# Norms of q and k by way of DRAM: the heads' sums spread over 128 partitions for root and reciprocal, and read back as rows

## The chip, the cores and the metric
One core of a Trainium2 chip runs the whole kernel. The metric is device microseconds (us) from start to end; 1604.22 us is the median of three runs before the change.

The engines are PE (TensorE: matmuls; PEld is its weight load), DVE (VectorE), ACT (ScalarE), POOL (GpSimd) and SP (SyncE, which here only issues DMAs). Each takes its instructions strictly in the order of the program; an instruction that waits holds everything behind it on its engine.

## The reference, cut to what matters
Two layers of a hybrid block over 256 latent and 256 context tokens. Each layer projects the normed tokens to an SSD branch, a neighbourhood attention and a gated MLP, merges the three, and ends with a SwiGLU FFN. The change touches the norms of q and k ahead of the attention: 8 heads of 64 channels, each head of each token normed by itself.

```
def rmsnorm(t, w):
    tf = t.astype(jnp.float32)
    tf = tf * lax.rsqrt(jnp.mean(tf * tf, axis=-1, keepdims=True) + EPS)
    return tf.astype(t.dtype) * w

def qkv_heads(t, q_norm, k_norm):
    q, k, v = [u.reshape(Bt, L, NA_HEADS, NA_HEAD_DIM) for u in split_cols(t, (NA_WIDTH,) * 3)]
    return rmsnorm(q, q_norm), rmsnorm(k, k_norm), v
```

All arithmetic is fp32. Layer 0 needs q and k of all 512 tokens, layer 1 (the last) k of all and q of the 256 latent ones.

## The kernel before, in words
Activations lie as channels on partitions and tokens along the free dimension: a tile `T()` is 128 channels by 512 tokens, fp32, and all such tiles share one pool of `N_T` buffers. A tile of q or k holds one pair of heads (64 partitions each), so four tiles hold all eight heads.

Every fp32 product is made of three matmuls in fp32r: each weight tile is split into a high part (`hi`, a cast on ACT, L222) and a remainder (`lo`, a subtraction on DVE, L232), each activation likewise, and `mm3` or `product` adds hi*hi, hi*lo and lo*hi in PSUM. Nearly all matmuls are therefore recorded at line L126, the helper `mm`; the tile names tell them apart (g is a projection's PSUM tile, s that of a small product).

The weights are one stream of 316 tiles of 512 KB. `Stream.get` keeps `hi` two tiles ahead of PE and `lo` one to two; after each `lo`, SP issues the load of the tile three further on (`load_to`, L212) into one of five raw buffers, and waits until that buffer is free.

The order of the instructions is written out by the program as it is traced. PE's projections are the backbone: every four tiles of k (12 matmuls) `gemm` calls `tick`, which lets side work take steps. There are three queues of side work, each a list of generators: "ssd" (the state space branch), "att" (the gated MLP's mixing, the norms of q and k, then the attention) and "mod" (the next modulation vectors). One `yield` is one step; the rate of "att" is 1.0 step a tick until all q, k and v are projected. Work can also be put off by a part of a tick (`later`).

`qk_tile` projects one tile of q or k, copies it from PSUM and squares it on ACT. When the four tiles of one kind are there, `qk_norm(kind)` is put into the "att" queue: once for k and once for q in each layer, four norms in all. `Q_0`, `Q_1` and `Q_2` are numbers of steps that it lets pass, (1, 2), (3, 5) and (6, 3) for layers 0 and 1.

Before the change a norm runs so: four groups of matmuls (L1073) sum the squares of each pair's two heads; pair j's sums land on the 32 partitions from 32j on (repeated, even heads and odd heads alternating). ACT takes the root of the whole 128 x 512 tile (L1076 for q, L1078 for k), DVE the reciprocal in halves of 256 columns, one step of the queue apart (L1081). After `Q_1` steps the result is split into an fp32r part and a remainder held on other partitions (L1086 on ACT, L1087 on DVE), so that one fp32r matmul restores it. After `Q_2` more steps, one step apart for each pair, a matmul with the 0/1 matrix `selp` (L1092, recorded at L126) spreads the pair's two rows over 64 partitions each, in PSUM, and DVE multiplies (L1094).

Two other paths through DRAM exist already and are used below as measures: `Fd` and `Cd` are small DRAM tiles written from the tile R (L869, L871) and read back as rows repeated over partitions, `rb` (L888, 128 partitions) and `ex` (L956, twice 64 partitions of 2 KB).

The attention, which reads q and k first in `stack` (L1109), is put into the queue when the "ssd" queue's last group has ended.

Of the kernel before, what the change touches and what calls it, by code (L numbers as in the profile page):

```python
# [9 lines left out]
F32 = mybir.dt.float32  # L10
F32R = mybir.dt.float32r
BF16 = mybir.dt.bfloat16
AF = mybir.ActivationFunctionType
ALU = mybir.AluOpType
AX = mybir.AxisListType
MUL, ADD, SUB, MAX, MIN = ALU.mult, ALU.add, ALU.subtract, ALU.max, ALU.min
# [17 lines left out]
C_ROW = 1280  # L34
C_BS = 1312
C_SP = 1344
# [2 lines left out]
C_MB = 1488  # L39
NC_ = 1616  # L40

N_T = 61
N_W = 5
LA = 2
N_WARM = 34
# [50 lines left out]
def kernel(ctx: ExitStack, tc: tile.TileContext, a, out):  # L96
    nc = tc.nc
    ctx.enter_context(tc.manual_schedule())
    PE, ACT, DVE, SP = nc.tensor, nc.scalar, nc.vector, nc.sync

    cpool = ctx.enter_context(tc.tile_pool(name="const", bufs=1))
    lpool = ctx.enter_context(tc.tile_pool(name="layer", bufs=2))
    tpool = ctx.enter_context(tc.tile_pool(name="t", bufs=N_T))
    rpool = ctx.enter_context(tc.tile_pool(name="raw", bufs=5))
# [3 lines left out]
    dpool = ctx.enter_context(tc.tile_pool(name="dram", bufs=1, space=bass.MemoryType.DRAM))  # L108
# [3 lines left out]
    def nm(s):  # L112
        cnt[0] += 1
        return f"{s}{cnt[0]}"

    def T(s="t", dt=F32):
        return tpool.tile([128, TOK], dt, tag="t", name=nm(s))

    def S(s="s"):
        return pspool.tile([128, 512], F32, tag="p", name=nm(s))  # L120

    def small(w, tag, bufs=None):
        return spool.tile([128, w], F32, tag=tag, name=nm(tag), bufs=bufs)

    def mm(o, l, r, start=True, stop=True):
        PE.matmul(o, l, r, start=start, stop=stop)  # L126


    cst = cpool.tile([128, C_MF], F32, name="cst")
# [12 lines left out]
    epsb, eps4, eps64 = (eps3[:, i:i + 1] for i in range(3))  # L142
    for e, f in ((epsb, 1.0), (eps4, 4.0), (eps64, 64.0)):
        DVE.memset(e, f * EPS)
    mk = cpool.tile([128, 256], F32, name="mk")
    selp = cpool.tile([128, 8, 128], F32R, name="selp")
    lom = cpool.tile([128, 1], F32, name="lom")
    ident = cst[:, C_ID:C_ID + 128]
    ones = cst[:, C_ONE:C_ONE + 128]

# [124 lines left out]
    def gemm(acts, c0, c1=512, la=LA):  # L275

        nk = len(acts)
        ps = S("g")
        for k, act in enumerate(acts):
            wh, wl = ws.get(pos[0] + k, la=la)  # L280
            product(ps, wh, wl, act, c0, c1, k == 0, k == nk - 1)
            if k % KT == KT - 1 or k == nk - 1:
                tick((k % KT + 1) / 4 * (c1 - c0) / 512)
        pos[0] += nk
        return ps
# [89 lines left out]
    def table(func):  # L375

        ACT.activation(dummy, epsb, func)


    class SumSq:  # L380
# [32 lines left out]
        def spread(self, c0, c1):  # L413

            if self.rs is None:
                self.rs = S("rs")
            for i in range(c0 // 128, c1 // 128):
                mm(self.rs[:, i * 128:i * 128 + 128], self.st[:, i:i + 1].to_broadcast([128, 128]), ident)
            return self.rs
# [74 lines left out]
    for k in range(8):  # L494
        t = T("x")
# [21 lines left out]
    h = [(T("hh", F32R), T("hl", F32R), 0) for _ in range(8)]  # L517
# [87 lines left out]
    for l in range(NL):  # L605
# [5 lines left out]
        def pcol(c, n=1):  # L611
            return P[:, c:c + n]
# [24 lines left out]
        for i in range(4):  # L637
            if last:
                t, c = ysc.norm(pl[i])
                ACT.activation(t[:, lat], t[:, lat], AF.Gelu_apprx_tanh, bias=c)  # L640
            else:
                t = T("u")
                ACT.activation(t, pl[i], AF.Gelu_apprx_tanh)
            u.append(t)
        if not last:
            SP.dma_start(out=cst[:, 0:C_ONE], in_=a["cst"][:, 0:C_ONE])
            SP.dma_start(out=cst[:, C_COS:C_ROW], in_=a["cst"][:, C_COS:C_ROW])
            SP.dma_start(out=cst[:, C_BS:C_MF], in_=a["cst"][:, C_BS:C_MF])
            SP.dma_start(out=mk, in_=a["cst"][:, C_MF:NC_])
            DVE.tensor_copy(selp.rearrange("p a (b c) -> p a b c", c=64),  # L650
                            cst[:, C_SP:C_SP + 16].rearrange("p (a b) -> p a b", b=2).unsqueeze(3).to_broadcast(
                                [128, 8, 2, 64]))

            DVE.tensor_reduce(out=lom, in_=cst[:, C_ROW + 4:C_ROW + 8], op=ADD, axis=AX.X)
            DVE.tensor_scalar(lom, lom, -1.0, None, MUL)

        def token_major(n0, evac, between=()):

# [113 lines left out]

        Fd = dpool.tile([64, 2, 128], F32, name=nm("Fd"))
        Cd = dpool.tile([16, 4, 128], F32, name=nm("Cd"))

        def pair_rows(j, pr):

            return selp[:, 2 * j + pr]

        def dt_gen():  # L780
            for _ in range(D_0[l]):
# [284 lines left out]
        def qk_norm(kind):  # L1066

            b = 0 if kind == "k" else c0
            for _ in range(Q_0[l]):
                yield  # L1070
            ps = S()
            for j in range(4):
                mm(ps[32 * j:32 * j + 32, b:], cst[:, C_BS:C_BS + 32], qsq.pop((kind, j))[:, b:])  # L1073
            rq, RQ = T("rq"), T("RQ", F32R)
            if kind == "q":
                ACT.activation(rq[:, b:], ps[:, b:], AF.Sqrt, bias=eps64)  # L1076
            else:
                ACT.activation(rq[:, b:], ps[:, b:], AF.Sqrt, scale=1.0 / 64, bias=epsb)  # L1078
            table(AF.Exp)
            for c in range(b, 512, 256):  # L1080
                DVE.reciprocal(rq[:, c:c + 256], rq[:, c:c + 256])  # L1081
                yield
            for _ in range(Q_1[l]):
                yield

            ACT.copy(RQ[:, b:], rq[:, b:])  # L1086
            DVE.scalar_tensor_tensor(RQ[:, b:], RQ[:, b:].bitcast(F32), lom, rq[:, b:], MUL, ADD)  # L1087
            for _ in range(Q_2[l]):
                yield
            for j in range(4):  # L1090
                ps = S()
                mm(ps[:, b:], pair_rows(j, 0), RQ[:, b:])  # L1092
                t = qk[kind, j]
                DVE.scalar_tensor_tensor(t[:, b:], t[:, b:], pcol(P_KN if kind == "k" else P_QN),  # L1094
                                         ps[:, b:], MUL, MUL)
                yield

        def attention():
# [173 lines left out]
        for g in range(4):  # L1272
            tiles = (g, 4 + g, 8 + 2 * g, 9 + 2 * g)
            if g < 2:
                for j, i in enumerate(tiles):
                    conv_tile(i)
                    qk_tile(j, "kq"[g])
            else:
                conv_tile(tiles[0])
                v_half(g - 2, [lambda: conv_tile(tiles[1])])  # L1280
                conv_tile(tiles[2])
                conv_tile(tiles[3])
            later(L_G[l], lambda g=g: queues["ssd"].append(ssd_group(g)))
            if g < 2:
                queues["att"].append(qk_norm("kq"[g]))
# [41 lines left out]
        for j in range(8):  # L1327
            ps = gemm(h, c0)
            t = T("z")
# [39 lines left out]
        h = None  # L1369
# [41 lines left out]
        for m in range(3, 8):  # L1411
            ps = gemm(mx, c0)
# [83 lines left out]
        if not last:  # L1496
# [9 lines left out]
            for m in range(8):  # L1506
                if m == 7:
                    drain("mod")
                    ysc = Scaled(xn, modA1, l + 1, 0)
                    ps = S("g")  # L1510
# [9 lines left out]
                else:  # L1520
                    ps = gemm(f, 0)
# [4 lines left out]
            h = [(T("hh", F32R), T("hl", F32R), 0) for _ in range(8)]  # L1526
            ysc.add()
        else:
            for m in range(8):

                ps = gemm(f if m < 7 else [tuple(z) for z in f], 256)
# [138 lines left out]
def _build(nc, arrays):  # L1670
    aps = {k: nc.dram_tensor(f"in_{k}", v.shape, mybir.dt.from_np(v.dtype), kind="ExternalInput").ap()
           for k, v in arrays.items()}
    out = nc.dram_tensor("out_0", (128, 8, 256), F32, kind="ExternalOutput").ap()
    with tile.TileContext(nc) as tc:
        kernel(tc, aps, out)
# [12 lines left out]
```

## Time and profile before

| | |
|---|---|
| runs, median of 3 (lowest, highest) | 1604.22 us (1604.22, 1604.6) |
| profiled execution, own time | 1605.74 us |
| its span, first to last instruction | 1603.7 us |
| granted TensorE clock, mean | 0.997 |
| PE busy | 1581.2 us, 99% |
| PEld busy | 1324.2 us, 83% |
| DVE busy | 1162.3 us, 72% |
| ACT busy | 830.3 us, 52% |
| DMA: moved, mean rate | 254.37 MB, 159 GB/s |

Busy time is the sum of the instructions' times on an engine. Matmuls overlap in their pipeline, so what a matmul costs PE is read from the start of one to the start of the next, not from its own duration. "Idle before it" of an instruction is time in which its engine stood still, and the name behind it is what released it; "issue" is time for which the profile shows no such event. A stretch A:B is in us from the span's start. The k norm of layer 0 stands at about 138 to 196 us and its q norm at 195 to 257 us; in layer 1 they stand at about 1098 to 1149 and 1162 to 1208 us.

### The profile page before, as it was taken

Reading aid. Unit: us, or ns where it says so; the run is one execution under the profiler, and the core shown is the slowest. Engines: PE = TensorE matmul, PEld = TensorE weight load, DVE = VectorE, ACT = ScalarE, POOL = GpSimd, SP = SyncE. Lnnn points to the kernel's source line nnn. Section 1 sums busy time; section 2 is a strip of 40 time slices with the busy share of each in tenths; the row PEclk is TensorE's granted clock in tenths of the full one; section 3 lists DMA queues with packets and bytes.
Section 4 is the critical chain, followed back from the end, with each engine's and each line's share of the span. In section 5 each row is a group of like instructions: output and inputs, shape, how many; then the busy total and the mean of one; then the engine's idle time right before and its main releaser. Section 6 shows DMA issues by size and latency. Waiting matters only on the chain.

```text
span 1603.7 us, 23594 instructions
## 1 busy us (share of the span) xinstructions
PE 1581.2 (99%) x8908; PEld 1324.2 (83%) x8909; DVE 1162.3 (72%) x2005; ACT 830.3 (52%) x1551; POOL 6.9 (0%) x21
## 2 busy tenths in 40 slices
PE   9999999999999999999999999999999999999999
PEld 5878787767788888988888888978888989998888
DVE  5477889878968656666666654778988987687664
ACT  4456876646743234433222212658676775566652
POOL 0000000000000000000000000000000000000000
PEclk9999999999999999999999999999999999999999
DMA  9523333443344445455456765425434455656654
GB/s 347 190 61 122 115 107 107 154 153 99 113 130 127 157 144 178 133 171 166 162 184 206 261 231 177 171 93 161 132 118 138 140 158 178 204 163 196 187 173 135
DMA packets 87345, 254.37 MB, mean 159 GB/s; under 512 B 10560, under 2 KB 19008, under 8 KB 87104
## 3 DMA queue, kind: packets, MB, share of 16 engines
q1 hardware_dynamic: 87232, 252.87, 49.3%
q8 instruction: 70, 1.15, 0.3%
q14 instruction: 43, 0.35, 0.1%
HBM read 248.44 MB, written 4.39 MB: 158 GB/s over the span
## 4 chain that ended last, share of the span: by engine, by line
PE 78%; DVE 11%; ACT 5%; DMA 4%; issue 2%; SPq 0%; ACTq 0%; DVEq 0%
PE g L126 70%; PE s L126 6%; DVE lo L232 3%; DVE xbc L718 2%; DMA wm<-in_wmod 1%; ACT hi L222 1%; DMA rb<-Fd 1%; PE s L1186 1%; ACT M L987 1%; DVE scr L192 1%; DMA wr<-in_ws 1%; DVE bt L1141 0%; DVE M L896 0%; ACT rb L987 0%; ACT sw L740 0%
## 5 line engine op out<-in xcount | busy, mean ns | idle before, releaser
L126 PE MATMUL g<-hh,hi 128*128 128x512 f32 (+1 forms) x1280 | 471.0, 368 | 0.0
L126 PE MATMUL g<-hh,lo 128*128 128x512 f32 (+1 forms) x1280 | 462.0, 361 | 1.4 <-DVE lo L232 1.4
L126 PE MATMUL g<-hl,hi 128*128 128x512 f32 (+1 forms) x1280 | 461.8, 361 | 0.5 <-DVE hl L551 0.4
L232 DVE TENSOR_TENSOR lo<-wr,hi 128x1024 fp32r<-128x1024 f32 x316 | 382.5, 1219 | 92.9 <-ACT hi L222 92.7
L222 ACT CAST hi<-wr 128x1024 fp32r<-128x1024 f32 x316 | 323.7, 1046 | 38.8 <-DMA wr<-in_ws 36.0
L126 PEld LDWEIGHTS g<-hh,hi 128*128 128x128 f32 x1280 | 241.5, 189 | 48.7 <-issue 11.9
L126 PEld LDWEIGHTS g<-hh,lo 128*128 128x128 f32 x1280 | 241.5, 189 | 41.1 <-DVE lo L232 3.8
L126 PEld LDWEIGHTS g<-hl,hi 128*128 128x128 f32 x1280 | 241.7, 189 | 37.2 <-DVE hl L551 1.1
L192 DVE SCALAR_TENSOR_TENSOR scr<-wm,csil 128x1024 bf16<-128x1024 f32 x128 | 156.1, 1220 | 55.4 <-DMA wm<-in_wmod 55.4
L126 PE MATMUL g<-hp,hi 128*128 128x512 f32 x304 | 107.6, 399 | 0.0
L718 DVE SCALAR_TENSOR_TENSOR xbc<-g,pv,xbc 128x508 f32<-128x508 f32 (+3 forms) x128 | 91.3, 713 | 9.5 <-ACT xbc L712 6.4
L126 PE MATMUL g<-hp,lo 128*128 128x256 f32 x304 | 85.6, 282 | 0.9 <-DVE lo L232 0.8
L1295 ACT ACTIVATE th<-g,pv 128x512 f32<-128x512 f32 (+1 forms) x48 | 27.9, 581 | 95.3 <-PE g L126 89.6
L367 ACT CAST fh<-f 128x512 fp32r<-128x512 f32 x22 | 13.6, 620 | 112.3 <-DVE f L1446 112.3
L126 PE MATMUL g<-fh,lo 128*128 128x512 f32 x176 | 68.6, 390 | 0.5 <-DVE lo L232 0.5
L126 PEld LDWEIGHTS g<-hp,hi 128*128 128x128 f32 x304 | 57.1, 188 | 14.1
L126 PE MATMUL g<-fh,hi 128*128 128x512 f32 x176 | 68.5, 389 | 0.0
L126 PE MATMUL g<-fl,hi 128*128 128x512 f32 x176 | 68.5, 389 | 0.0
L126 PE MATMUL g<-lo,hh 128*128 128x256 f32 x224 | 63.6, 284 | 3.2 <-DVE lo L232 3.1
L126 PE MATMUL g<-hi,hh 128*128 128x256 f32 x224 | 64.6, 288 | 0.0
L126 PE MATMUL g<-hi,hl 128*128 128x256 f32 x224 | 63.3, 283 | 0.0
L126 PE MATMUL g<-fp,hi 128*128 128x512 f32 (+1 forms) x198 | 62.4, 373 | 0.0
(310 smaller groups left out, 2658.2 us busy)
## 6 DMA issues: line engine op xcount, KB each, us to landing
wr<-in_ws SPq DMA_DIRECT2D x316, 512.0 KB, 4.2
wm<-in_wmod SPq DMA_DIRECT2D x80, 512.0 KB, 4.5
rb<-Fd SPq DMA_DIRECT2D x48, 256.0 KB, 4.0
wm<-in_wm SPq DMA_DIRECT2D x32, 256.0 KB, 6.0
ex<-Cd SPq DMA_DIRECT2D x32, 128.0 KB, 3.8
bias<-in_rpb SPq DMA_DIRECT2D x32, 128.0 KB, 2.1
x<-in_xT SPq DMA_DIRECT2D x8, 256.0 KB, 5.1
xm<-in_xT SPq DMA_DIRECT2D x8, 256.0 KB, 5.5
```

The lines of the kernel that those rows point to most:

```text
L126: PE.matmul(o, l, r, start=start, stop=stop)
L192: DVE.scalar_tensor_tensor(scr, raws[n], 1.0, csil[:, v, :], MUL, MUL, accum_out=modr[l][:, ft, v:v + 1])
L222: ACT.copy(hi, self.raw[i])
L232: DVE.tensor_tensor(lo, self.raw.pop(i), hi, SUB)
L367: ACT.copy(hi, src[:, c0:])
L718: DVE.scalar_tensor_tensor(av3[:, :, o0:o1], pv3[:, :, o0 + d:o1 + d], w(j), av3[:, :, o0:o1], MUL, ADD)
L987: ACT.activation(z, z, AF.Exp, bias=bias(st, d))
L1186: PE.transpose(ps[:, kt * 256 + qt * 128:kt * 256 + qt * 128 + 128], src, ident)
L1295: ACT.activation(th[:, c0:], ps[:, c0:], AF.Tanh, scale=0.5, bias=pcol(P_BG + br * 8 + m))
```

## The change
The heads' sums of squares are copied from PSUM by ACT and written to a DRAM tile `Nd` of 8 heads by n tokens (n is 512, or 256 for q in layer 1), two rows from each group of 32 partitions. They are read back flat as `w`, 128 partitions by n/16 values. After `Q_1` steps the root (ACT) and the reciprocal (DVE) are taken of `w`, which is written to a second DRAM tile `Ni`. `spread(j)` reads the two rows of a pair back, each repeated on 64 partitions, with two DMAs into an SBUF tile; pair 0's is issued at once, pair j+1's just ahead of pair j's multiplication. The multiplication reads that tile in place of PSUM. The matmuls with `selp`, the split into two parts, `selp` and `lom` themselves and their set-up are gone, and so is the step between the two halves of the reciprocal. The tile pool has one buffer more (4 KB of `selp` are free).

```diff
-N_T = 61
+N_T = 62
...
-    selp = cpool.tile([128, 8, 128], F32R, name="selp")
-    lom = cpool.tile([128, 1], F32, name="lom")
...
-            rq, RQ = T("rq"), T("RQ", F32R)
-            if kind == "q":
-                ACT.activation(rq[:, b:], ps[:, b:], AF.Sqrt, bias=eps64)
-            else:
-                ACT.activation(rq[:, b:], ps[:, b:], AF.Sqrt, scale=1.0 / 64, bias=epsb)
-            table(AF.Exp)
-            for c in range(b, 512, 256):
-                DVE.reciprocal(rq[:, c:c + 256], rq[:, c:c + 256])
-                yield
+
+            n = 512 - b
+            t, w = T("rq"), small(32, "rqs", 2)
+            Nd, Ni = (dpool.tile([8, n], F32, name=nm("Nd")) for _ in range(2))
+            ACT.copy(t[:, b:], ps[:, b:])
+            for j in range(4):
+                SP.dma_start(out=Nd[2 * j:2 * j + 2], in_=t[32 * j:32 * j + 2, b:])
+            flat = lambda z: z.rearrange("h t -> (h t)").rearrange("(p c) -> p c", p=128)
+            w = w[:, 0:n // 16]
+            SP.dma_start(out=w, in_=flat(Nd))
             for _ in range(Q_1[l]):
                 yield
-
-            ACT.copy(RQ[:, b:], rq[:, b:])
-            DVE.scalar_tensor_tensor(RQ[:, b:], RQ[:, b:].bitcast(F32), lom, rq[:, b:], MUL, ADD)
+            if kind == "q":
+                ACT.activation(w, w, AF.Sqrt, bias=eps64)
+            else:
+                ACT.activation(w, w, AF.Sqrt, scale=1.0 / 64, bias=epsb)
+            table(AF.Exp)
+            DVE.reciprocal(w, w)
+            SP.dma_start(out=flat(Ni), in_=w)
+            R = {}
+
+            def spread(j):
+                R[j] = T("RQ")
+                for a_ in (0, 1):
+                    SP.dma_start(out=R[j][64 * a_:64 * a_ + 64, b:],
+                                 in_=Ni[2 * j + a_].unsqueeze(0).to_broadcast([64, n]))
+
+            spread(0)
             for _ in range(Q_2[l]):
                 yield
             for j in range(4):
-                ps = S()
-                mm(ps[:, b:], pair_rows(j, 0), RQ[:, b:])
                 t = qk[kind, j]
+                if j < 3:
+                    spread(j + 1)
                 DVE.scalar_tensor_tensor(t[:, b:], t[:, b:], pcol(P_KN if kind == "k" else P_QN),
-                                         ps[:, b:], MUL, MUL)
+                                         R.pop(j)[:, b:], MUL, MUL)
                 yield
```

## Rows read from the trace of the kernel before

**Rows 1.** Page, part 1: busy us, share of the span, instructions by engine.
```profile
PE 1581.2 (99%) x8908; PEld 1324.2 (83%) x8909; DVE 1162.3 (72%) x2005; ACT 830.3 (52%) x1551; POOL 6.9 (0%) x21
```
**Rows 2.** Page, part 4: the chain that ended last, by engine.
```profile
PE 78%; DVE 11%; ACT 5%; DMA 4%; issue 2%; SPq 0%; ACTq 0%; DVEq 0%
```
**Rows 3.** Stretches: length, then busy us of each engine, clock, DMA share, GB/s.
```profile
150.00:176.00 26.00, 26.00 (x115) 20.24 (x114) 19.50 (x34) 19.20 (x46) 0.00 (x0) 1.00 0.56 174
176.00:192.00 16.00, 16.00 (x77) 11.94 (x76) 15.76 (x27) 13.98 (x35) 0.00 (x0) 1.00 0.43 146
200.00:230.00 30.00, 30.00 (x175) 24.64 (x174) 26.09 (x43) 22.12 (x57) 0.00 (x0) 1.00 0.36 109
230.00:250.00 20.00, 17.82 (x104) 14.39 (x103) 19.35 (x30) 12.65 (x28) 0.00 (x0) 1.00 0.50 154
...
1098.00:1130.00 32.00, 31.19 (x192) 26.36 (x192) 29.36 (x47) 28.79 (x64) 0.00 (x0) 1.00 0.64 198
```
**Rows 4.** Tile RQ: count, ns min/median/max, first and last start, forms.
```profile
L126 PE MATMUL s<-RQ,selp x16: 278/486/580, 176.5 to 1206.2; 128*128 128x512 f32 x12, 128*128 128x256 f32 x4
...
L1087 DVE SCALAR_TENSOR_TENSOR RQ<-RQ,lom,rq x4: 476/742/752, 158.4 to 1186.1; 128x512 fp32r<-128x512 f32 x3, 128x256 fp32r<-128x256 f32 x1
```
**Rows 5.** Timeline of PE: start us, us, instruction.
```profile
176.53 0.58 PE L126 MATMUL s<-RQ,selp 128*128 128x512 f32 x1
...
180.82 0.50 PE L126 MATMUL s<-RQ,selp 128*128 128x512 f32 x1
...
181.16 0.40 PE L126 MATMUL g<-hh,hi 128*128 128x512 f32 x1
...
1199.60 0.28 PE L126 MATMUL s<-RQ,selp 128*128 128x256 f32 x1
...
1199.72 0.40 PE L126 MATMUL g<-hh,hi 128*128 128x512 f32 x1
```
**Rows 6.** Timeline: matmuls that PE waited for; idle time and releaser in brackets.
```profile
198.58 0.39 PE L126 MATMUL g<-lo,hh 128*128 128x256 f32 x1 [0.93 <-DVE lo L232]
...
244.91 0.38 PE L126 MATMUL g<-lo,hh 128*128 128x256 f32 x1 [2.18 <-DVE lo L232]
...
253.23 0.47 PE L126 MATMUL s<-RQ,selp 128*128 128x512 f32 x1 [1.34 <-DVE xbc L718]
...
1130.64 0.50 PE L126 MATMUL g<-hh,lo 128*128 128x512 f32 x1 [0.78 <-DVE lo L232]
```
**Rows 7.** Groups on DVE by form: busy us, mean ns, idle before, releaser.
```profile
L730 DVE SCALAR_TENSOR_TENSOR xbc<-ct,xbc 128x512 f32<-128x512 f32 x28 | 19.1, 682 | 0.0
L1081 DVE RECIPROCAL rq<-rq 128x256 f32<-128x256 f32 x7 | 12.2, 1747 | 3.6 <-ACT rq L1078 3.0 <-ACT rq L1076 0.6
...
L1094 DVE SCALAR_TENSOR_TENSOR k<-k,pv,s 128x512 f32<-128x512 f32 x8 | 5.9, 740 | 0.0
...
L1148 DVE RECIPROCAL ast<-ast 128x2 f32<-128x2 f32 x16 | 2.5, 158 | 0.3 <-ACT bt L1144 0.3
```
**Rows 8.** Tile ex, read from DRAM: issue ns on SP, and time to landing.
```profile
L956 SPq DMA_DIRECT2D ex<-Cd x32: 450/587/1480, 160.7 to 1233.1; - x32
...
DMA to landing us min/median/max: 2.7/3.8/8.8
```
**Rows 9.** Tile R, written to DRAM in twelve DMAs: time to landing.
```profile
DMA to landing us min/median/max: 1.4/1.6/1.9
```
**Rows 10.** Timeline of layer 0's k norm: the sums, and the cast five steps later.
```profile
138.61 1.06 PE L126 MATMUL s<-sq,cst 128*32 128x512 f32 x8
...
156.17 0.62 ACT L1086 CAST RQ<-rq 128x512 fp32r<-128x512 f32 x1
```
**Rows 11.** SP's waits in 130:260: us in total, times, longest us.
```profile
SPq L212 <- DVE lo L232: 33.7, 7, 9.4
...
SPq L869 <- ACT R L867: 10.4, 1, 10.4
```
**Rows 12.** Line L1109 in 0:700, the attention's first read of k.
```profile
L1109 ACT CAST ks<-k x8: 610/616/621, 347.3 to 422.8; 64x512 fp32r<-64x512 f32 x8
```

More of the change, by code (lines that the diff above doesn't have):

```diff
@@ L649 @@
             SP.dma_start(out=mk, in_=a["cst"][:, C_MF:NC_])
[L650 to L655, printed above, removed]
         def token_major(n0, evac, between=()):
@@ L774 @@
         Cd = dpool.tile([16, 4, 128], F32, name=nm("Cd"))
-        def pair_rows(j, pr):
-            return selp[:, 2 * j + pr]
         def dt_gen():
```

## The prediction, made before the changed kernel ran
> **What bounds the kernel now.** I began with the busy times: PE is busy 99% of the span, DVE 72% [rows 1]. The chain that ended last says the same, 78% PE, but 11% of it is DVE [rows 2], so DVE must end PE's waits somewhere. The table of stretches shows where. From 176 us on, where layer 0's projections, its SSD groups and these norms run side by side, DVE is busy 15.76 of 16 us, 26.09 of 30 and 19.35 of 20, while PE drops to 17.82 of 20 in the last of these; in layer 1's k norm it is 29.36 of 32 for DVE [rows 3]. The timeline then gives the single waits of PE next to the norms: 0.93, 2.18 and 0.78 us for the remainder of a weight tile, which DVE makes, and 1.34 us of a matmul of the norm itself for a PSUM bank that DVE's convolution taps held [rows 6]. So near the norms there are two bounds close together: PE nearly everywhere, DVE just behind it, and in front at four places worth 5.2 us.
>
> **PE, on the path.** Sixteen matmuls with the selector go, 12 of 512 columns and 4 of 256 [rows 4]. Their durations overlap with their neighbours, so I count from start to start: the one at 180.82 us moves the next matmul to 181.16, that is 0.34 us; a narrow one at 1199.60 moves it to 1199.72, 0.12 us [rows 5]. All sixteen, read that way, lie between 0.12 and 0.36. For the wide ones I take 0.28, for the narrow ones 0.15: 12 x 0.28 + 4 x 0.15 = 4.0 us. The bounds are 16 x 0.12 = 1.9 and 16 x 0.34 = 5.4 us. The sums of squares stay as they are.
>
> **DVE, partly on the path.** A norm of 512 columns loses two reciprocals of 1.747 us [rows 7] and the remainder of 0.742 [rows 4], 4.24 us. It gains one reciprocal of 128 x 32. The profile has 0.158 us for 128 x 2 and 1.747 for 128 x 256 [rows 7]; a straight line between them gives 0.35. The four multiplications read SBUF in place of PSUM; today they take 0.740, and the same operation on SBUF tiles 0.682 (L730) [rows 7], so 0.23 is saved. Net -4.1 us in three norms and about half, -2.1, in layer 1's q: 14.4 us in all. Of that only what ends a wait of PE counts. The 2.18 and the 1.34 us stand late in layer 0's q norm, behind its 4.1 us; the 0.78 stands behind both reciprocals of layer 1's k norm. The 0.93 at 198.58 stands behind multiplications only, and I leave it. So 4.3 us could go, from nothing to all. I take half, 2.2 us, because the new multiplications may wait (below) and because the PSUM bank is wanted by the next product anyway.
>
> **ACT.** A copy replaces the root on the wide tile, a root on a small tile is added, and the cast goes; table loads stay the same in number. That is no more work than before, on an engine with 2 us free in the tightest stretch of 16 [rows 3]: nothing. If the small root has to wait for its data, though, ACT stops, and with it the emptying of PSUM.
>
> **Is `w` there in time?** Copy (about as long as the cast, 0.62 us [rows 10]), four issues on SP, the write's landing, one more issue, the read's landing. With 0.59 us an issue [rows 8], 1.6 for the write [rows 9], and for the read between 1.6 [rows 9] and 3.8 [rows 8] it is 0.6 + 4 x 0.59 + 1.6 + 0.6 + 1.6 to 3.8 = 6.8 to 9.0 us. The cover is Q_1 steps. Layer 0's k norm took five steps from 138.61 to 156.17 [rows 10], 3.5 us each, so three are 10.5 us. It fits by 1.5 us at the narrowest place; layer 1 has five steps. Cost: nothing, and up to 2 us where SP is late.
>
> **SP.** Each norm puts 14 DMAs into the queue that also carries the weights and the SSD rows: 14 x 0.59 = 8.3 us of issue, and two places where SP stands until a DMA of its own has landed, 1.6 us each. Behind them stand weight loads (L212) and the rows rb. The weights have room: in this part SP itself stood 33.7 of 130 us waiting for DVE to free a raw buffer [rows 11]. It has stood before without harm to PE: 10.4 us for the tile R [rows 11], and PE behind it is busy 26.00 of 26 [rows 3]. [...] The rows rb can come later by about two landings; ACT waits for them just once today. I put 0.6 us on this, from 0 to 3.2 (two landings in the one norm, layer 0's k, in which the first rows are fetched).
>
> **Is the spread there in time?** Pair 0's has the Q_2 steps. Pair j+1's is issued one step ahead of its use; steps here are 180.82 - 176.53 = 4.3 us [rows 5], about 4.0 without the matmul. Two issues and a landing like ex, which has exactly this shape, are 2 x 0.59 + 3.8 = 5.0 us [rows 8]. Where SP is level with DVE in the program, DVE waits 1.0 us for it; where SP is ahead, nothing. Twelve such spreads, half of them late: 6 us of DVE, well below the 14.4 that it gains. [...]
>
> **Latency of the norm.** It ends two steps earlier in the program, and k and q of layer 0 are first read at 347.3 us [rows 12], some 90 us after the last multiplication. Hidden; the buffer more and the dropped set-up of `selp`, three DVE instructions once in the whole run, I put at nothing.
>
> **Sum.** -4.0 - 2.2 + 0.6 = -5.6 us. The profiled execution took 1605.74 us around a span of 1603.7; it would become 1600.1. The median of the runs is 1.5 us lower, 1604.22, so I predict 1598.6 us. What a measurement can tell from no change is 0.2%, or 3.2 us: 1601.0 to 1607.4.
>
> **Rivals.**
> More goes: all four waits of PE end, as DVE's 14.4 us would allow. -4.0 - 5.2 = -9.2, 1595.0 us. For it: the waits are short beside what DVE is relieved of. Against it: each wait that goes may show the next one, and spreads cost DVE time.
> DVE stays the bound in layer 0: the eight wide matmuls there are worth 8 x 0.28 = 2.2 us, and PE meets DVE again where they were. None of the waits goes: -4.0 + 2.2 = -1.8, 1602.4 us, no change to be measured. For it: 19.35 of 20 us of DVE. Against it: DVE loses more work there than PE does.
> Slower, by late spreads: the landing of ex reaches 8.8 us [rows 8], and with 1 MB more a norm in a stretch with a DMA share of 0.43 to 0.56 [rows 3] a landing midway, 6.2 us, is possible. Then each spread is late by 1.2 + 6.2 - 4.0 = 3.4 us, three of them 10.2 a norm, less the 4.1 gained: 6.1 us net. In layer 0's q norm DVE has no room and PE takes it all; in its k norm the 6.5 us that DVE has free in 150:176 [rows 3] swallow it; in layer 1's k norm 2.6 us are free and 3.5 pass. 6.1 + 3.5 - 4.0 = +5.6, 1609.8 us. It begins where three late spreads eat the relief: at a landing of 4.0 - 1.2 + 4.1 / 3 = 4.2 us. Against it: the median is 3.8, SP is often ahead of DVE, and DVE shows no wait for ex today.
>
> **How the numbers follow.** Forecast 0.54 (own range 1595.5 to 1601.5), more goes 0.10, DVE stays the bound 0.20, slower 0.16. The forecast's upper end reaches a little into no change; the rest there comes from the third case. Faster 0.62, same 0.22, slower 0.16. The range 1593.5 to 1607.0 takes in the first three cases, the bounds of the matmuls and of the waits, and the lighter half of the slow one.
>
> **What would show it.** No matmul with RQ, and the sixteen steps on PE gone; DVE's busy time down by some 14 us; the waits of 2.18, 1.34 and 0.78 us shorter or gone; no wait of ACT for `w`; DVE's waits for the tile RQ under 1 us each; weight casts on ACT waiting no more for their loads than before. A wait of several us of DVE for RQ with a remainder of a weight tile behind it, or of ACT for `w`, would prove me wrong; so would PE's waits coming back elsewhere between 260 and 380 us with the same total.

## The result, and the profile after

The changed kernel is slower: 1614.21 us in the median (1613.34 to 1617.62, four runs) against 1604.41 for the kernel before, a ratio of 1.0065, 95% interval 1.0052 to 1.0078 (it isn't the quotient of the two medians, which is 1.0061). The forecast was 1598.6 us with a range up to 1607.0; the rival that ended slower had 1609.8, by a mechanism that did not occur. The profiled execution took 1614.59 us around a span of 1612.8, 9.1 us more than before.

First the page of the kernel after, busy us by engine, then its chain of waits:

```profile
PE 1582.6 (98%) x8892; PEld 1326.8 (82%) x8893; DVE 1148.7 (71%) x1995; ACT 829.7 (51%) x1551; POOL 6.9 (0%) x21
```
```profile
PE 79%; DVE 10%; ACT 4%; DMA 4%; issue 2%; SPq 1%; DVEq 0%; ACTq 0%
```

Against [rows 1] DVE has 13.6 us less, close to the 14.4 forecast, and PE has its 16 matmuls less. Yet PE's busy time is 1.4 us longer, its idle time 7.7 (30.2 against 22.5), and the kernel 9.1. The work went as planned; its place did not. The stretches show where [rows 3] (length, then busy us of PE, PEld, DVE, ACT and POOL, granted clock, DMA share, GB/s):

```profile
150.00:176.00 26.00, 26.00 (x118) 20.36 (x117) 17.48 (x30) 21.88 (x50) 0.00 (x0) 1.00 0.65 199
176.00:192.00 16.00, 15.37 (x72) 11.14 (x71) 15.79 (x26) 12.68 (x34) 0.00 (x0) 1.00 0.54 171
200.00:230.00 30.00, 28.87 (x167) 24.53 (x169) 20.26 (x34) 18.14 (x42) 0.00 (x0) 0.94 0.39 123
230.00:250.00 20.00, 16.31 (x83) 12.65 (x79) 17.88 (x29) 14.34 (x36) 0.00 (x0) 0.97 0.53 158
1098.00:1130.00 32.00, 31.32 (x194) 26.68 (x193) 23.26 (x38) 25.41 (x56) 0.00 (x0) 1.00 0.51 150
```

In 200:230 DVE is busy 20.26 us where it was 26.09, and still PE has lost 1.1 us. DVE is idle for 10 us there, and in the next stretch PE waits for it. PE's waits near the norms, from the timeline (start, us, instruction; in brackets the idle time ahead and what released it):

```profile
201.13 0.58 PE L126 MATMUL g<-lo,hh 128*128 128x256 f32 x1 [2.00 <-DVE lo L230]
252.55 0.58 PE L126 MATMUL g<-lo,hh 128*128 128x256 f32 x1 [6.24 <-DVE lo L230]
1132.73 0.50 PE L126 MATMUL g<-hh,hi 128*128 128x512 f32 x1 [1.13 <-ACT hi L220]
1136.00 0.50 PE L126 MATMUL g<-hh,lo 128*128 128x512 f32 x1 [2.54 <-DVE lo L230]
1187.71 0.58 PE L126 MATMUL g<-lo,hh 128*128 128x256 f32 x1 [2.95 <-DVE lo L230]
```

Where [rows 6] had 0.93, 2.18 and 0.78 us for `lo` there are 2.00, 6.24 and 2.54, and two new ones, 1.13 us for `hi` in layer 1's k norm and 2.95 in its q norm. Only the 1.34 us for a PSUM bank went, with its matmul. So the engine that was relieved is later than before. What made it late stands on ACT, just behind layer 0's k norm; ACT's timeline:

```profile
150.66 0.59 ACT L915 COPY xt<-s 128x512 f32<-128x512 f32 x1
151.27 1.28 ACT L1077 ACT_TABLE_LOAD   x1
152.56 0.32 ACT L1077 ACTIVATE rqs<-rqs,eps 128x32 f32<-128x32 f32 x1
152.90 1.28 ACT L375 ACT_TABLE_LOAD   x1
154.20 0.20 ACT L375 ACTIVATE dummy<-eps 128x1 f32<-128x1 f32 x1
154.41 1.65 ACT L732 COPY sw<-xbc 32x256 f32<-32x256 f32 x4
```

The small root, with the table's change to it and back, takes 3.1 us (151.27 to 154.41), and the copies `sw` of the SSD branch come that much later. ACT's timeline in the kernel before:

```profile
137.61 1.28 ACT L1078 ACT_TABLE_LOAD   x1
139.77 0.69 ACT L1078 ACTIVATE rq<-s,eps 128x512 f32<-128x512 f32 x1 [0.88 <-PE s L126]
140.48 1.28 ACT L377 ACT_TABLE_LOAD   x1
...
150.05 1.65 ACT L740 COPY sw<-xbc 32x256 f32<-32x256 f32 x4
```

There the first load lay in time that ACT spent waiting for the sums, and `sw` followed right behind `xt`. Of the 4.4 us between 150.05 and 154.41, 1.2 stand ahead of every norm (the table below), and 3.1 are the block. And DVE in the kernel after, on its timeline, stands in front of the reciprocal all that while, with a weight's remainder and the `sw` work behind it:

```profile
152.92 0.35 DVE L1079 RECIPROCAL rqs<-rqs 128x32 f32<-128x32 f32 x1 [5.79 <-ACT rqs L1077]
153.19 1.16 DVE L230 TENSOR_TENSOR lo<-wr,hi 128x1024 fp32r<-128x1024 f32 x1
156.09 0.42 DVE L733 TENSOR_TENSOR xbc<-xbc,cst 128x256 f32<-128x256 f32 x1 [1.74 <-ACT sw L732]
```

SP stands too. Its waits over the whole run (us in total, times, longest):

```profile
SPq L1080 <- DVE rqs L1079: 41.9, 4, 14.9
SPq L1068 <- ACT rq L1066: 34.2, 4, 11.3
SPq L1086 <- DMA Nd<-rqs: 4.3, 4, 1.1
SPq L1071 <- DMA Nd<-rq: 4.2, 5, 1.5
```

The longest, 14.9 us, is the write of the reciprocals in layer 0's q norm. Behind it, on the queue's timeline, come the weights and the SSD rows, all at once:

```profile
216.53 0.33 SPq L1080 DMA_DIRECT2D Nd<-rqs  x1
218.00 1.93 SPq L1086 DMA_DIRECT2D RQ<-Nd  x2
219.99 0.58 SPq L210 DMA_DIRECT2D wr<-in_ws  x1
220.61 1.38 SPq L876 DMA_DIRECT2D rb<-Fd  x3
```

Before, the four `rb` of this group were issued one by one, from 201.68 to 220.93 us. The chain of waits runs through just these: the table load at 214.50, the root, the reciprocal, the write's landing (1.41 us), the spread's issue, and 5.88 us for `rb`.

To put a place to the loss, take the same remainder `lo` in both traces and subtract its start before from its start after. The first column is where every profile stands ahead of any norm (executions differ by 0.5 to 1.9 us in the first 30 us, the kernels taken from before too); the others have that offset taken off. Worked out from start times, us; all rows but the first are the experiments below. Each row is one execution, and executions of one kernel lie up to 6 us apart over the whole run (wide root: 1599.05 to 1604.95), so a difference of one us in one row proves little by itself:

| start in the kernel before | 137.62 | 149.03 | 191.94 | 224.75 | 243.64 | 342.01 | 1085.42 | 1129.37 | 1239.48 |
|---|---|---|---|---|---|---|---|---|---|
| after | 1.21 | 2.95 | 2.00 | 5.09 | 6.43 | 1.26 | 1.03 | 4.15 | 8.71 |
| wide root | 1.67 | -0.24 | -0.01 | -1.36 | -0.02 | -3.91 | -5.35 | -5.19 | -2.64 |
| DMAs on POOL | 1.06 | 2.95 | 2.02 | 3.03 | 4.37 | -0.66 | -1.16 | 1.98 | 3.08 |
| spare tables in the kernel before | 0.54 | -0.01 | 1.48 | 5.96 | 5.99 | 5.78 | 5.31 | 5.31 | 5.28 |
| after, 61 buffers | 1.94 | 2.95 | 2.03 | 3.12 | 4.48 | 2.94 | 3.45 | 6.56 | 12.65 |
| spare tables beside the wide root | 1.61 | -0.24 | 1.86 | 4.25 | 5.58 | 0.78 | 0.42 | 3.44 | 10.93 |
| reciprocal a step later | 1.51 | -1.04 | 2.20 | 4.67 | 5.35 | 1.28 | -0.42 | 2.96 | 3.20 |
| both (wide root, DMAs on POOL) | 1.91 | -0.23 | -0.02 | -1.91 | -0.33 | -4.18 | -2.95 | -2.78 | -3.47 |
| wide root, nine DMAs on POOL | 1.86 | -0.25 | -0.04 | -1.91 | -0.34 | -5.53 | -5.86 | -5.72 | -3.16 |

The kernel after loses 2.0 us in layer 0's k norm, 4.4 more in its q norm, gains 5.2 back between 244 and 342 us, loses 3.1 in layer 1's k norm and 4.6 in its q norm.

### The profile page after: what moved, and what is told of

Read it like the earlier page. It is cut to its first block, busy times and chain, and to the rows that moved or that the text cites. A ratio compares the mean times of both kernels' runs of the same rounds, so it can differ in the third digit from the quotient of the medians.

```text
span 1612.8 us, 23636 instructions
## 1 busy us (share of the span) xinstructions
PE 1582.6 (98%) x8892; PEld 1326.8 (82%) x8893; DVE 1148.7 (71%) x1995; ACT 829.7 (51%) x1551; POOL 6.9 (0%) x21
## 4 chain that ended last, share of the span: by engine, by line
PE 79%; DVE 10%; ACT 4%; DMA 4%; issue 2%; SPq 1%; DVEq 0%; ACTq 0%
PE g L126 71%; PE s L126 6%; DVE lo L230 2%; DMA wm<-in_wmod 2%; DVE xbc L710 1%; ACT hi L220 1%; PE s L1188 1%; DVE scr L190 1%; DMA rb<-Fd 1%; DVE M L884 1%; DMA wr<-in_ws 1%; ACT M L975 0%; DVE bt L1143 0%; ACT sw L732 0%; DVE ks L1116 0%
## 5 line engine op out<-in xcount | busy, mean ns | idle before, releaser
L365 ACT CAST fh<-f 128x512 fp32r<-128x512 f32 x22 | 13.6, 620 | 112.9 <-DVE f L1448 112.9
```

The source lines that it names most:

```text
L365: ACT.copy(hi, src[:, c0:])
```

## Experiments

Theory A: the loss comes from the root's new place, since a root and two table loads on ACT now stand in the middle of the SSD work. Theory B: it comes from SP, which stands before its stores while weights and rows queue behind. All ratios are to the kernel before on the same chip, with 95% intervals.

### Root on the wide tile at its old place

```diff
-            ACT.copy(t[:, b:], ps[:, b:])
+            if kind == "q":
+                ACT.activation(t[:, b:], ps[:, b:], AF.Sqrt, bias=eps64)
+            else:
+                ACT.activation(t[:, b:], ps[:, b:], AF.Sqrt, scale=1.0 / 64, bias=epsb)
+            table(AF.Exp)
...
-            if kind == "q":
-                ACT.activation(w, w, AF.Sqrt, bias=eps64)
-            else:
-                ACT.activation(w, w, AF.Sqrt, scale=1.0 / 64, bias=epsb)
-            table(AF.Exp)
             DVE.reciprocal(w, w)
```


> The changed kernel with the root taken of the wide tile, straight from PSUM in place of the copy, and the table switch back to Exp right behind it, where the kernel before had them; only the reciprocal is left for the small tile. Theory A (the root's place: two table loads of 1.28 us and the two small activations, 3.1 us of ACT in all, now stand Q_1 steps later, between the SSD work's copies and exponentials, and make these and DVE's work behind them late): most of the loss goes, 1603 us, within 3, and PE's waits of 6.2 and 2.0 us for a weight remainder in layer 0 shrink below 2.5. Theory B (SP's order: the store of the reciprocals holds SP for 12 to 15 us a norm and the SSD rows and weights behind it): SP's wait stays, so the time stays at 1613, within 2.

0.9991 (0.9982 to 1.0001), 1602.86 us. The DRAM path, its 14 DMAs on SP and the waits of SP are still there (SP waits 34.4 us for the reciprocals, where it was 41.9); only root and tables have moved back, and the loss is gone. ACT and DVE behind layer 0's k norm (timelines; the second fence is DVE):

```profile
151.73 1.65 ACT L732 COPY sw<-xbc 32x256 f32<-32x256 f32 x4
```
```profile
149.11 0.34 DVE L1078 RECIPROCAL rqs<-rqs 128x32 f32<-128x32 f32 x1
```

No table load ahead of `sw`, no bracket at the reciprocal. Theory A is what holds; B can't be the larger part.

### The 14 DMAs on POOL

```diff
-                SP.dma_start(out=Nd[2 * j:2 * j + 2], in_=t[32 * j:32 * j + 2, b:])
+                nc.gpsimd.dma_start(out=Nd[2 * j:2 * j + 2], in_=t[32 * j:32 * j + 2, b:])
...
-            SP.dma_start(out=w, in_=flat(Nd))
+            nc.gpsimd.dma_start(out=w, in_=flat(Nd))
...
-            SP.dma_start(out=flat(Ni), in_=w)
+            nc.gpsimd.dma_start(out=flat(Ni), in_=w)
...
-                    SP.dma_start(out=R[j][64 * a_:64 * a_ + 64, b:],
+                    nc.gpsimd.dma_start(out=R[j][64 * a_:64 * a_ + 64, b:],
```


> The changed kernel with all fourteen DMAs of a norm issued from POOL's queue in place of SP's; roots stay where the change put them. Theory A: the table loads stand where they stood, 1612 us, within 3. Theory B: SP's waits for the copy and the reciprocal (34 and 42 us) are gone, rows and weights go out as before, and the time falls to 1602 us, within 3.

1.0034 (1.0019 to 1.0050), 1609.65 us: slower than before, as A has it, but 0.31% faster than the kernel after. In the table it parts from the kernel after at 224.75 (3.03 against 5.09) and again in layer 1's q norm (1.1 us lost between 1129 and 1239, against 4.6): SP had stood 14.9 us before a store in the one, and 11.3 and 12.1 in the other. In layer 1's k norm it had stood 12.9, and there both kernels lose 3.1: what counts is not how long SP stands, but what it holds up. Theory B is a true but smaller part.

### Both

The kernel with the wide root, and its DMAs on POOL as above:

```diff
-            SP.dma_start(out=flat(Ni), in_=w)
+            nc.gpsimd.dma_start(out=flat(Ni), in_=w)
...
```


> Both edits together: root on the wide tile at its old place, and the fourteen DMAs on POOL's queue. Both theories: 1600 us, within 3, since neither cause is left and sixteen matmuls (4 us) are saved. If it is still above 1606, a third cause is at work (buffers of the pool, the start).

0.9971 (0.9962 to 0.9981), 1598.95 us, faster than both kernels. The four ratios make a square: 1.0065, 0.9991 with the wide root, 1.0034 with POOL, 0.9971 with both. The root's place costs 0.0074 with SP and 0.0063 with POOL; SP's queue 0.0031 with the late root and 0.0020 with the early one. In us (times 1604) that is 10 to 12 and 3 to 5.

### The kernel before with the root moved behind the Q_1 steps

```diff
             rq, RQ = T("rq"), T("RQ", F32R)
+            ACT.copy(rq[:, b:], ps[:, b:])
+            for _ in range(Q_1[l]):
+                yield
             if kind == "q":
-                ACT.activation(rq[:, b:], ps[:, b:], AF.Sqrt, bias=eps64)
+                ACT.activation(rq[:, b:], rq[:, b:], AF.Sqrt, bias=eps64)
...
-            for _ in range(Q_1[l]):
-                yield
```


> The kernel before, without DRAM or spreads, in which only the root and its table switch move behind the Q_1 steps: a copy on ACT stands where the root stood, the root follows Q_1 steps later with the reciprocals. Theory A: slower than before by about 5 us or more, 1609 to 1614, with the same waits of PE in layer 0 and layer 1. Theory B: no change from before, 1604, within 2, since no DMA is added.

1.0091 (1.0076 to 1.0107), 1618.35 us, a little past the range. No DRAM and no added DMA, and the whole loss is there. But more than the root has moved: the wide reciprocals follow it, and ACT has one copy more in each norm, so the size is not that of the root's place alone. DVE on its timeline:

```profile
153.47 1.75 DVE L1084 RECIPROCAL rq<-rq 128x256 f32<-128x256 f32 x1 [6.20 <-ACT rq L1081]
```

### Two spare table loads, in the kernel before

What of it is ACT's own time, and what is DVE standing? Here root and reciprocals stay early, and two table loads that nobody waits for (3.0 us with their dummy activations) are put behind the Q_1 steps.

```diff
             for _ in range(Q_1[l]):
                 yield
+            table(AF.Sqrt)
+            table(AF.Exp)
...
             ACT.copy(RQ[:, b:], rq[:, b:])
```


> The kernel before, whole, with one thing added: after the Q_1 steps ACT switches its table to Sqrt and back to Exp (two table loads of 1.28 us and two activations of one column, 3.0 us), and nothing waits for it but what is behind it on ACT. Theory A1 (it is ACT's 3 us at that place that cost the time, by making the SSD's copies and exponentials late): 1609 to 1615 us. Theory A2 (it is the place of the reciprocals and of what DVE waits for): no change from before, within 2 us.

1.0040 (1.0026 to 1.0053), 1610.64 us. Two more loads at a bad place cost 6 us though only what is behind them on ACT waits for them. ACT's first load (the second is at 158.34), and then PE's longer wait in layer 0:

```profile
156.82 1.28 ACT L377 ACT_TABLE_LOAD   x1
```
```profile
251.44 0.58 PE L126 MATMUL g<-lo,hh 128*128 128x256 f32 x1 [5.22 <-DVE lo L232]
```

The 5.22 us at 251 is nearly the kernel after's 6.24. By the table the pairs cost 1.5 and 4.5 us in layer 0's two norms and next to nothing in layer 1. They do not stand where the kernel after has its root: the steps between the early reciprocals put them later, behind `sw` in layer 0's k norm. The next experiment has them at the root's own place.

### The same two loads beside the wide root

```diff
             for _ in range(Q_1[l]):
                 yield
+            table(AF.Sqrt)
+            table(AF.Exp)
             DVE.reciprocal(w, w)
```


> Root on the wide tile at its old place (all DMAs on SP), and after the Q_1 steps a switch of ACT's table to Sqrt and back that nothing but ACT's own queue waits for (3.0 us). Against the same kernel without the switch (0.9991 of before): if ACT's time at that place makes about half of the root's loss, 1.003 of before, from 1.002 to 1.0045; if it makes all of it, 1.0065 as in the changed kernel; if none, 0.999.

1.0051 (1.0033 to 1.0069), 1614.08 us, 0.6% over the kernel that it was made from. Its interval holds the whole loss (1.0065) and, of what was expected for half of it, only the upper end. ACT, DVE and PE on their timelines:

```profile
151.66 1.28 ACT L375 ACT_TABLE_LOAD   x1
```
```profile
149.05 0.35 DVE L1080 RECIPROCAL rqs<-rqs 128x32 f32<-128x32 f32 x1
```
```profile
252.10 0.58 PE L126 MATMUL g<-lo,hh 128*128 128x256 f32 x1 [5.53 <-DVE lo L230]
```

The loads stand where the kernel after has them, DVE waits at no reciprocal, and yet PE's waits are nearly those of the kernel after: 2.00, 5.53, 2.54 and 2.95 us against 2.00, 6.24, 2.54 and 2.95. By the table it loses 1.9 and 3.7 us in layer 0's two norms and 3.0 in layer 1's k norm; the kernel after lost 2.0, 4.4 and 3.1, the wide root without the loads 0.0, 0.0 and 0.2. So in these three norms ACT's own 3 us account for nearly the whole loss. In layer 1's q norm it loses more than the kernel after, 7.5 against 4.6.

### The reciprocal one step later

```diff
             table(AF.Exp)
+            yield
             DVE.reciprocal(w, w)
```


> The changed kernel with one step of the queue between the root on ACT and the reciprocal on DVE (and its store and first spread), so that DVE does not stand at the reciprocal until ACT, with its table load, has come to the root (5.8 us once in layer 0 of the changed kernel). If DVE's wait is the other half of the root's loss: 1.0035 of before, from 1.001 to 1.005, against 1.0065 of the changed kernel. If ACT's time alone counts: 1.0065, within 0.0015.

1.0024 (1.0013 to 1.0034), 1608.72 us: 0.4% of the kernel after's 0.65% is gone by one step, though ACT's loads are where they were. DVE on its timeline:

```profile
149.49 1.23 DVE L230 TENSOR_TENSOR lo<-wr,hi 128x1024 fp32r<-128x1024 f32 x1 [2.07 <-ACT hi L220]
156.36 0.43 DVE L733 TENSOR_TENSOR xbc<-xbc,cst 128x256 f32<-128x256 f32 x1 [5.64 <-ACT sw L732]
```

The idle time has hardly shrunk; it now stands at `sw`, and the reciprocal comes at 158.04. `lo` runs at 149.49 in place of 153.19, but layer 0's k norm gains nothing by it (2.20 us lost against 2.00), its q norm 1.3, and layer 1's k norm nothing (3.4 against 3.1). Most of the gain is layer 1's q norm, which loses 0.2 us in place of 4.6, and PE's wait of 2.95 us at 1187.71 no longer occurs. There it is SP's order that has changed. In the kernel after two of four `rb` go out behind the stores of the sums, and DVE waits for them (SP, then DVE):

```profile
1163.74 1.14 SPq L1068 DMA_DIRECT2D Nd<-rq  x4
1165.88 0.34 SPq L1071 DMA_DIRECT2D rqs<-Nd  x1
1166.32 1.09 SPq L944 DMA_DIRECT2D ex<-Cd  x2
1167.50 1.00 SPq L876 DMA_DIRECT2D rb<-Fd  x2
```
```profile
1171.37 0.69 DVE L884 TENSOR_TENSOR M<-rb,mk 128x512 f32<-128x512 f32 x1 [4.39 <-DMA rb<-Fd]
```

With the step, which puts off the q norm too, three of these four `rb` go out from 1149.58 to 1156.77, ahead of the stores at 1166.20, only one goes out behind them, and DVE has no such wait. So most of the 0.4% is not the price of DVE's standing. In the k norm of layer 1 DVE now waits 4.09 us for a spread, which the kernel after did not.

### 61 buffers in place of 62

```diff
-N_T = 62
+N_T = 61
```


> The changed kernel with 61 buffers in the tile pool in place of 62, all else as changed. Theory A and B: no change from the changed kernel, 1613 to 1614 us, within 2. A theory in which the other sharing out of the buffers costs the time: 1606 us or less.

1.0084 (1.0069 to 1.0099), 1619.02 us: not the 1614 expected. The interval overlaps that of the kernel after, so the 0.19% between them is not clear of noise, but the table has a place: between 243.64 and 342.01 the kernel after wins 5.2 us back, this one 1.5.

### POOL for the write of the reciprocals and the spreads

To the kernel with the wide root, for nine DMAs of the 14; the four stores of the sums' roots and the read of them stay on SP:

```diff
             DVE.reciprocal(w, w)
-            SP.dma_start(out=flat(Ni), in_=w)
+            nc.gpsimd.dma_start(out=flat(Ni), in_=w)
...
-                    SP.dma_start(out=R[j][64 * a_:64 * a_ + 64, b:],
+                    nc.gpsimd.dma_start(out=R[j][64 * a_:64 * a_ + 64, b:],
```


> The kernel with the root on the wide tile at its old place; of the fourteen DMAs a norm only the store of the reciprocals and the eight spreads go to POOL's queue, the four stores of the roots and their read stay on SP. If SP's loss is the wait for the reciprocal (42 us in the changed kernel) and for the store to land: 1599 us, within 2, as with all fourteen on POOL. If it is the wait for ACT's copy ahead of the first stores, or the number of issues: 1603 us, within 2, as with all on SP.

0.9981 (0.9972 to 0.9991), 1602.38 us, between the wide root alone (0.9991) and all DMAs on POOL (0.9971), with intervals that meet both; by the times it can't be told which of SP's waits costs what. The traces tell it for one place: in layer 1's q norm DVE waits 3.23 us for `rb` (at 1162.91) as with the wide root alone (3.23 at 1163.26), and the table has 2.6 us lost in both; with all fourteen on POOL there is no such wait, and 0.7 is gained. There it is the first stores that hold the rows up, not the write of the reciprocals.

### Both, and Q_2 longer

```diff
-Q_2 = (6, 3)
+Q_2 = (8, 5)
```


> Root on the wide tile, all fourteen DMAs on POOL's queue, and Q_2 two steps more in both layers, so that the multiplications stand about where they stood before the reciprocals' two steps went. If DVE's multiplications of q just ahead of a weight remainder make PE's last wait in layer 0 (3.0 us at 246 us of that kernel): that wait falls by 0.7 to 1.5 us and the time to 1597.5 us. If the wait comes from DVE's holes earlier on: no change, 1599 us, within 1.5.

0.9955 (0.9940 to 0.9970), 1598.16 us, the lowest ratio of all, though its interval overlaps that with Q_2 as it was (0.9962 to 0.9981). PE's wait at 245 us, first with Q_2 as it was, then with the longer one:

```profile
246.49 0.58 PE L126 MATMUL g<-lo,hh 128*128 128x256 f32 x1 [3.00 <-DVE lo L230]
```
```profile
245.06 0.39 PE L126 MATMUL g<-lo,hh 128*128 128x256 f32 x1 [2.10 <-DVE lo L230]
```

### Q_2 longer still

```diff
-Q_2 = (8, 5)
+Q_2 = (11, 8)
```


> As the version with the root on the wide tile, POOL's queue and Q_2 two steps more (0.9955 of before), with Q_2 five steps more than in the changed kernel, 11 and 8. If later multiplications only move DVE's work out of its tightest stretch: 0.9955 or down to 0.994. If they now meet the last SSD group or the attention: 0.997 or more.

0.9958 (0.9944 to 0.9973), 1598.7 us: no more is gained.

### The best version with 16 matmuls put back

```diff
             for j in range(4):
+                ps = S()
+                mm(ps[:, b:], h[1][0][:, 0:128], h[0][0][:, b:])
                 t = qk[kind, j]
```
Their results are not read; they take the place that the selector's matmuls had.

> The best version so far (root on the wide tile, POOL's queue, Q_2 two steps more; 0.9955 of before) with sixteen fp32r matmuls of the removed ones' sizes put back where they stood, each into a PSUM bank of its own that nobody reads. It measures the term for PE. As summed in the prediction, 4.0 us of TensorE: 0.9980 of before, from 0.9967 (1.9 us) to 0.9989 (5.4 us). If PE waits for DVE there anyway and the matmuls fit into the waits: 0.9955, within 0.001.

0.9968 (0.9959 to 0.9978), 1598.64 us: 0.13% or 2 us over the version without them, at the low end of what the forecast's 4.0 us with its bounds would give (0.9967 to 0.9989). The intervals overlap, so it isn't told apart from nothing. The term was more likely 2 than 4 us; settled it is not.

### The best version with 61 buffers

```diff
-N_T = 62
+N_T = 61
```


> The kernel with both causes taken away and the longer Q_2 (0.9955), with 61 tile buffers in place of 62. Theory A: the change's 62nd buffer is worth some 3.5 us, in the SSD group ahead of the attention of layer 0. There the same remainder of a weight tile falls from 6.8 to 2.5 us behind the kernel before when there are 62 buffers, and only from 5.8 to 4.9 with 61. Then this kernel is 0.22% slower than with 62: ratio 0.9977 (0.9966 to 0.9988), some 1601 us, and DVE again waits 1.3 to 2 us at a time for the rows rb between 320 and 345 us. Theory B: the buffer is worth nothing, as the prediction had it, and what was gained there came from the shorter work of DVE: ratio 0.9955 (0.994 to 0.997), and no waits for rb there.

0.9987 (0.9976 to 0.9998), 1602.25 us: 0.32% slower than with 62, at the upper edge of what was expected, and the two intervals don't meet. DVE's waits on its timeline:

```profile
326.45 0.69 DVE L884 TENSOR_TENSOR M<-rb,mk 128x512 f32<-128x512 f32 x1 [1.68 <-DMA rb<-Fd]
335.41 0.69 DVE L884 TENSOR_TENSOR M<-rb,mk 128x512 f32<-128x512 f32 x1 [1.71 <-DMA rb<-Fd]
339.35 0.69 DVE L884 TENSOR_TENSOR M<-rb,mk 128x512 f32<-128x512 f32 x1 [1.20 <-DMA rb<-Fd]
```

and the stretches there, first with 62 buffers, then with 61 (columns as above):

```profile
330.00:350.00 20.00, 20.00 (x96) 15.04 (x93) 19.72 (x35) 11.13 (x23) 1.04 (x2) 1.00 0.47 153
350.00:400.00 50.00, 49.83 (x266) 39.54 (x265) 43.83 (x98) 31.57 (x68) 2.25 (x5) 1.00 0.40 129
```
```profile
330.00:350.00 20.00, 19.74 (x93) 14.18 (x90) 16.08 (x26) 9.62 (x21) 1.04 (x2) 1.00 0.50 155
350.00:400.00 50.00, 47.53 (x244) 37.33 (x243) 43.35 (x99) 29.57 (x64) 2.08 (x4) 1.00 0.39 128
```

With 62 PE is busy 69.83 of 70 us, with 61 it is 67.27. The kernel before had 19.16 and 47.57 here, 66.73, and three waits of DVE for `rb` too, of 1.77 to 2.05 us. So one buffer is worth 0.32% here, some 5 us (0.19% or 3 us in the kernel after, where the intervals overlap), of which 2.6 are seen as PE's idle time; with it the rows `rb` are there in time ahead of the attention (with 62 buffers no wait of DVE for them stands there). In the kernel after it hid a part of the loss, and of the best version's 0.45% it is the larger part: without it, the DRAM path at its best is worth 0.13%, or 2 us.

## Why the prediction was wrong

**The step that failed is ACT's: "That is no more work than before [...] nothing."** The work was counted rightly: busy 829.7 against 830.3 us. Its place was not. Before, the loads stood around the norm's own sums, where ACT in layer 0 waited for PE in any case (0.88 and 2.33 us before the two roots); after, they stand Q_1 steps on, in three of the four norms straight ahead of the copies `sw` that the SSD groups need at once. In layer 1 ACT didn't wait for the sums before either; why the old place is cheap there too (0.2 us in its k norm with the wide root, against 3.1) isn't shown. "2 us free in the tightest stretch of 16" said nothing of that, since the block of 3.1 us made `sw`, right behind it, 3.1 us late on an engine that is busy 21.88 of 26 us in 150:176. The sentence that came near, that ACT would stop if the root had to wait for its data, looked at the wrong wait: `w` was always there. With the wide root, 10 to 12 us of the loss are gone.

A load takes 1.28 us on ACT's timeline of the kernel after; the first one starts 0.02 us behind the copy ahead of it and the root 0.01 us behind the load. So the cost that has to be placed is the measured 3.1 us for both switches and the root.

**The wait at the reciprocal was not listed.** The prediction asked who waits for a late `w`, and for late spreads, but not who stands behind a reciprocal that waits for ACT. DVE stood 5.79 us once, with `lo` behind it, and 1.0 to 1.4 us in the other norms. But little of the loss is shown to come of it: without it, the spare loads beside the wide root lose nearly as much in three of the four norms, and what one step more gave back (0.4%) came for the most part from SP's order in the fourth. So ACT's own 3 us at that place are the larger part of the root's 0.63 to 0.74%; the spare loads alone cost 0.4 to 0.6%. The exact share is left open, as the two overlap.

**SP, 0.6 us (0 to 3.2): too small.** Measured 3 to 5 us. The issues were cheaper than taken (a write of a sums' row 0.25 us, a spread 0.46, against 0.59), the waits for a landing about as taken (at most 1.1 and 1.5 against 1.6). But the sum priced SP's time and the landings, and not that SP, in order, stands before a store until DVE has done it: 41.9 us for four. Of the 10.4 us that [rows 11] had for R it was argued that PE didn't mind; R is the SSD's own tile: the rows behind it are read from R's stores and couldn't have gone out sooner, (of two weight loads that stood there too, at 150.89, PE took no harm), while the rows behind the norm's stores have nothing to do with these. The other queue was worth 0.20 to 0.31%, because there a store that waits for compute (14.9 us at the longest in the kernel after) is not in front of the loads.

**DVE's relief, -2.2 us: not found.** The 13.6 us of work did go, the reciprocal took 0.354 us as worked out, and the multiplication from SBUF 0.745, no less than the 0.740 from PSUM, where a saving of 0.06 was taken. But with both causes taken away PE's wait that was to shrink, 2.18 us, is 3.00. In that kernel DVE is still busy 19.65 of 20 us in 230:250: the relief came at other times, and a multiplication that was left (244.56) stands right ahead of the `lo` that PE wanted (245.22). Moving the multiplications two steps on took 0.9 us from that wait; that it took time from the kernel isn't clear of noise.

**PE, -4.0 us.** The matmuls are gone, and with both causes taken away PE's busy time is 1578.4 us, 2.8 less than before. Put back they cost 2 us, not clear of noise; the term was, if anything, half of the size forecast. The reading behind it was loose too: from one start to the next the sixteen lie between 0.12 and 0.42 us, not 0.36, and add up to 5.0, not 4.0.

**The buffer, "at nothing": a gain of 3 to 5 us** (only the 5 clear of noise), mis-sized the other way; without it the ratio was 1.0084. The prediction looked for waits for `rb` on ACT alone ("just once today"); DVE waited for them three times between 324 and 341 us, 5.7 us in all, and these waits are gone.

**What was right:** no wait of ACT for `w`, no wait of DVE for a spread (the slower rival lived on these and did not occur; that it had the direction right is luck), and the norm's latency hidden.

The sum from the runs: the change with the root at its old place and its DMAs on POOL is -0.29% (of which the buffer is 0.19 to 0.32, and the rest 0.1 at most), SP's queue adds 0.20 to 0.31, the root's place 0.63 to 0.74.

## What to carry to other kernels

A change that kept the number of table loads cost 10 to 12 us here by where they stand: read who is next on that engine at the new place, as the block of 3.1 us made `sw` behind it 3.1 us late though ACT was busy only 51% of the span. For each instruction that is moved behind a wait, ask on each engine, the DMA queue too, what stands behind the one that now waits (here `lo` behind DVE's 5.79 us, weights and rows behind SP's 14.9); put helper stores that wait for compute, all of them, on a queue that carries no loads (0.20 to 0.31% here). And a freed buffer was not nothing (0.32% in the best version): try it by itself, lest its gain be credited to, or hide, the rest.

## What the runs showed of the hardware

Around PE's waits near the norms the granted clock fell in the kernel after: in 195:205, 240:260, 1125:1145 and 1180:1200 us it is 0.83, 0.83, 0.91 and 0.91 on the mean, and 1.00 in the kernel before. In the wait of 6.24 us it fell while PE stood: 1.00 in 246:248, 0.74 in 248:250 and 0.50 in 250:252. Behind that wait, on PE's timeline:

```profile
252.93 0.41 PE L126 MATMUL g<-hi,hl 128*128 128x256 f32 x1
253.14 0.41 PE L126 MATMUL g<-hi,hh 128*128 128x256 f32 x1
```

Such matmuls start 0.21 us apart here, at a granted clock of 0.50 (253:255); in the kernel before, behind its wait of 2.18 us, they started 0.12 apart, at 1.00. From the second matmul to the next product it takes 2.26 us (252.93 to 255.19) in place of 1.27: this wait cost 1 us on top of its idle time. PE's busy time, 1.4 us longer with 16 matmuls less, agrees with that. The same length of wait didn't always have it: behind 2.18 us in the kernel before the clock stayed at 1.00 (244:247), behind 2.10 us in the best version it fell 0.3 us after PE had begun again (0.85 in 244:246, 0.50 in 246:248), and behind the 2.00 us at 201.13 of the kernel after it fell as PE began again (0.58 us for the first matmul; 0.58 in 201:202, 0.50 in 202:204). What decides, these runs don't tell.
